# Two of four weight sums of a seven-product block scheme: from VectorE additions to accumulating transfers

## The chip, the cores and the metric

The kernel runs on one core of a Trainium2 chip. The metric is the device time of one execution in microseconds (us). The kernel before was run three times: 1967.50, 1963.14 and 1965.54 us, median 1965.54 us. One more execution was recorded by the hardware profiler; all rows below come from it.

The engines are named as the profile names them: PE (TensorE, matrix products), PEld (its weight loads), DVE (VectorE), ACT (ScalarE), POOL (GpSimd) and SP (SyncE, which here only issues transfers). A small q behind a name means the engine's queue of instructions rather than its datapath.

## What is computed

A decoder trunk of two layers on one sequence of 512 tokens with 1024 channels, in float32. Each layer adds three terms to x:

```
x += 0.5 * swiglu(rmsnorm(x), ffn1_w_in, ffn1_w_out)
x += mixer(rmsnorm(x))
x += 0.5 * swiglu(rmsnorm(x), ffn2_w_in, ffn2_w_out)

def _swiglu(x, w_in, w_out):
    gate, up = jnp.split(x @ w_in, 2, axis=-1)
    return (jax.nn.silu(gate) * up) @ w_out
```

The inner width of the feed-forward part is 2816. The mixers (a convolution beside sparse attention in the first layer, a short convolution beside stick-breaking attention in the second) are not touched by the change. A last norm ends the trunk. So there are four feed-forward parts, and the change lies in their second product, with `w_out`.

## The kernel before, in words

**Products in two halves.** Every float32 operand of a product is split into a rounded part and a rest (`split`, L87 to L94): ACT writes the rounded part (L90, or L93 with a factor), DVE subtracts it from the source (L91 or L94). `mm3` (L119 to L122) then issues three matmuls for each pair of 128 by 128 weights and a slab of activations. So each weight block costs one ACT pass, one DVE pass and a run of matmuls.

**The feed-forward part** (`ffn`, L248). Its inner width is 22 tiles of 128, taken in 11 pairs. `up(s)` computes one pair: four weight tiles of 512 KB come in by `load_w` (L103, three raw buffers, three buffers for each split half), 96 matmuls of 512 columns fill the banks `gu`, and DVE and ACT make the activation from them. The product with `w_out` takes three pairs at a time (`CHUNKS`), each in two halves of the output channels (`down(c0, n, q)`, L274). That is six calls of `seven` in each feed-forward part, 24 in the program. Between two calls stands at least one `up`. The last two pairs go through a plain product (`down_tail`).

**`seven`** (L211) multiplies a two by two block matrix in seven products instead of eight, Strassen's scheme in Winograd's form. The four weight blocks 11, 12, 21 and 22 of 384 KB each are loaded by SP into buffers `rb` (six of them, L220). DVE forms four weight sums in buffers `ws` (two of them) and in place:

```
s[1] = raw["21"] + raw["22"]         # L237, product 5
s[2] = s[1] + raw["11"]              # L238, product 6 (with the sign turned)
raw["21"] = raw["11"] + raw["21"]    # L240, product 7
s[2] = s[2] + raw["12"]              # L244, product 3
```

The products are written in the order 1, 2, 6, 7, 5, 4, 3; each splits its weights and issues 18 matmuls of 256 columns into the banks `px`, `py` and `pw`, and after each DVE adds the bank to the residual x (`taps`, L285).

**What sets the order of the work.** The program is written in the order above, but each engine's instructions are put in order at build time by a scheduler that simulates the engines: an instruction of lower rank (later in the program) goes ahead where a simulated engine has nothing earlier that is ready. Each engine then runs its list strictly in order. A buffer of a group (`rb`, `ws`, `raw`, `whi`, `wlo`) is handed out again when its last reader is done, and the loads of a later set are placed as soon as buffers are free. So SP, DVE and ACT work on the next call of `seven` while PE still works on the present one. POOL has little to do: in the feed-forward parts it adds squares for the next norm (`Norm.square`, L170), at the very start and beside the last plain products.

Of the kernel before, what the change touches and what calls it, by code (L numbers as in the profile page):

```python
# [11 lines left out]
ALU = mybir.AluOpType  # L12
# [22 lines left out]
S_11, S_21, S_22, S_T1, S_T3, S_T2, S_T4 = 1, 2, 3, 4, 5, 6, 7  # L35
# [17 lines left out]
def trunk(ctx: ExitStack, tc: tile.TileContext, a: dict, out: bass.AP):  # L53
    nc = tc.nc
    V, S, G, PE = nc.vector, nc.scalar, nc.gpsimd, nc.tensor
# [11 lines left out]
    def nm(s):  # L67
        n_name[0] += 1
        return f"{s}_{n_name[0]}"
# [17 lines left out]
    def split(hi, lo, src, scale=None):  # L87

        if scale is None:
            S.activation(hi, src, AF.Copy)  # L90
            V.tensor_tensor(lo, src, hi, ALU.subtract)  # L91
        else:
            S.activation(hi, src, AF.Copy, scale=scale)  # L93
            V.scalar_tensor_tensor(lo, src, scale, hi, op0=ALU.mult, op1=ALU.subtract)  # L94
# [24 lines left out]
    def mm3(o, wh, wl, xh, xl, start, stop, **kw):  # L119
        PE.matmul(o, wh, xh, start=start, stop=False, **kw)  # L120
        PE.matmul(o, wh, xl, start=False, stop=False, **kw)  # L121
        PE.matmul(o, wl, xh, start=False, stop=stop, **kw)  # L122
# [89 lines left out]
    def seven(ph, blocks, n, ops, taps):  # L212

        w = 2 * n * P
        raw = {}
        for b in ("11", "12", "22", "21"):
            raw[b] = ph.tile("rb", "rb", 768)[:, :w]
            nc.sync.dma_start(raw[b], blocks[b])  # L220
        s = {i: ph.tile("ws", "ws", 768)[:, :w] for i in (1, 2)}
        X, Y, W = (ph.bank(t, t) for t in ("px", "py", "pw"))

        def product(name, o, src, op, first, sign=None):
            hi = wsp.tile([P, 1024], F32R, tag="whi", name=nm("whi"))[:, :w]
            lo = wsp.tile([P, 1024], F32R, tag="wlo", name=nm("wlo"))[:, :w]
            split(hi, lo, src, sign)
            for k in range(n):
                for j in range(2):
                    sl = slice((j * n + k) * P, (j * n + k + 1) * P)  # L230
                    mm3(o[:, j * TH:(j + 1) * TH], hi[:, sl], lo[:, sl], *ops[k][op],
                        first and k == 0 and j == 0, k == n - 1, skip_group_check=True)
            taps(name, o)

        product("1", X, raw["11"], S_11, True)
        product("2", Y, raw["12"], S_21, True)
        V.tensor_tensor(s[1], raw["21"], raw["22"], ALU.add)  # L237
        V.tensor_tensor(s[2], s[1], raw["11"], ALU.add)  # L238
        product("6", X, s[2], S_T2, False, -1.0)
        V.tensor_tensor(raw["21"], raw["11"], raw["21"], ALU.add)  # L240
        product("7", W, raw["21"], S_T3, True)
        product("5", X, s[1], S_T1, False)
        product("4", W, raw["22"], S_T4, False)
        V.tensor_tensor(s[2], s[2], raw["12"], ALU.add)  # L244
        product("3", X, s[2], S_22, False)

    def ffn(norm, w_in, w_out, w_tail, nxt, ph, last=None):
# [30 lines left out]
        def down(c0, n, q):  # L278

            m0 = 4 * q  # L280

            def taps(m, o):
                r, c = {"1": (0, 0), "2": (0, 0), "6": (1, 0), "7": (1, 1), "5": (1, 1), "4": (1, 0), "3": (0, 1)}[m]
                x = xT[:, m0 + 2 * r:m0 + 2 * r + 2, c * TH:(c + 1) * TH]
                V.scalar_tensor_tensor(x, halves(o), -0.5 if r else 0.5, x, op0=ALU.mult, op1=ALU.add)  # L285

            w = 2 * n * P
            blocks = {b: w_out[q, i, :, 2 * c0 * P:2 * c0 * P + w] for i, b in enumerate(("11", "21", "12", "22"))}
            seven(ph, blocks, n, [act[c0 + k] for k in range(n)], taps)
# [569 lines left out]
    def early_w(n, c):  # L859
        sl = slice(c * T, (c + 1) * T)  # L860
        nc.sync.dma_start(first[n][:, sl], a["w1_in"][0][0, :, n, sl])
        return sp[n][0][:, sl], sp[n][1][:, sl], first[n][:, sl]

    order = {0: [(0, 0), (1, 0)], 2: [(0, 1)], 3: [(1, 1)]}
    for k in range(KD):
        nc.sync.dma_start(xT[:, k, :], a["x"][k])
        ws = [early_w(*nc_) for nc_ in order.get(k, ())]
# [175 lines left out]
```

## Time and profile before

| what | value |
|---|---|
| three runs | 1963.14 to 1967.50 us, median 1965.54 |
| profiled execution | 1965.56 us |
| its span, first to last instruction | 1963.8 us |
| PE busy | 1930.6 us (98%) |
| DVE busy | 1322.0 us (67%), 1973 instructions |
| ACT busy | 790.1 us (40%) |
| POOL busy | 104.1 us (5%), 112 instructions |
| moved by transfers | 178.02 MB, mean 91 GB/s |

How to read it: a busy share tells which engine has work all the time, not which one ends last at a given place. Matmuls are pipelined, so two neighbours overlap in the rows and the time of one is longer than the distance between two starts. The profiled execution lasted 1.76 us longer than its span.

### The profile page before, as it was taken

How to read it: one execution, taken by the hardware profiler on the slowest of the kernel's cores; microseconds unless marked ns; L12 is line 12 of the kernel's file. 1: busy time of each engine (PE TensorE's matmuls, PEld its weight loads, DVE VectorE, ACT ScalarE, POOL GpSimd, SP SyncE). 2: the span in 40 equal slices, each digit the busy share in tenths (PEclk: the TensorE clock that was granted, in tenths of full speed). 3: DMA queues.
4: the chain of work that ended last, by engine and by line, in shares of the span. 5: the costliest groups of instructions: out<-in, count | busy, mean ns of one | idle time of the engine just before them, and what ended most of it. 6: DMA issues, size and time to landing. Idle time of an engine off the chain costs nothing.

```text
span 1963.8 us, 25263 instructions
## 1 busy us (share of the span) xinstructions
PE 1930.6 (98%) x10128; PEld 1632.0 (83%) x10128; DVE 1322.0 (67%) x1973; ACT 790.1 (40%) x1129; POOL 104.1 (5%) x112
## 2 busy tenths in 40 slices
PE   8999999989999999999999999999999999999997
PEld 6888989878667888888988888888877888888896
DVE  6566757699986656666675666656578655666664
ACT  5333323436685433333343333334545433333333
POOL 2000000100232100000010000001000110000001
PEclk9999999999999999999999999999999999999999
DMA  6233331332100432323233333322321243232311
GB/s 220 94 91 102 92 102 52 100 103 82 43 1 28 150 97 84 113 82 117 86 111 96 97 97 98 98 80 75 94 67 55 77 143 97 84 114 81 117 52 54
DMA packets 53972, 178.02 MB, mean 91 GB/s; under 512 B 5984, under 2 KB 6368, under 8 KB 53856
## 3 DMA queue, kind: packets, MB, share of 16 engines
q1 hardware_dynamic: 53712, 176.29, 28.7%
q8 instruction: 79, 1.29, 0.3%
q14 instruction: 37, 0.30, 0.0%
q10 hardware_dynamic: 144, 0.14, 0.0%
HBM read 174.30 MB, written 2.10 MB: 90 GB/s over the span
## 4 chain that ended last, share of the span: by engine, by line
PE 97%; DVE 1%; ACT 1%; issue 0%; DMA 0%; DVEq 0%; SPq 0%; ACTq 0%
PE gu L120 16%; PE gu L121 16%; PE gu L122 16%; PE px L120 4%; PE px L122 4%; PE px L121 4%; PE ac L120 3%; PE ac L122 3%; PE ac L121 3%; PE pw L122 2%; PE pw L121 2%; PE pw L120 2%; PE fo L120 2%; PE fo L121 2%; PE fo L122 2%; PE mo L121 1%
## 5 line engine op out<-in xcount | busy, mean ns | idle before, releaser
L120 PE MATMUL gu<-xh,whi 128*128 128x512 f32 x1408 | 549.7, 391 | 8.3 <-ACT whi L90 6.1
L121 PE MATMUL gu<-xl,whi 128*128 128x512 f32 x1408 | 549.9, 391 | 0.0
L122 PE MATMUL gu<-xh,wlo 128*128 128x512 f32 x1408 | 546.4, 390 | 0.0
L90 ACT ACTIVATE whi<-raw 128x1024 fp32r<-128x1024 f32 (+2 forms) x256 | 268.9, 1051 | 565.3 <-PE gu L121 188.7
L91 DVE TENSOR_TENSOR wlo<-raw,whi 128x1024 fp32r<-128x1024 f32 (+2 forms) x256 | 312.8, 1222 | 55.0 <-ACT whi L90 51.0
L120 PEld LDWEIGHTS gu<-xh,whi 128*128 128x128 f32 x1408 | 265.5, 189 | 62.6 <-ACT whi L90 6.3
L122 PEld LDWEIGHTS gu<-xh,wlo 128*128 128x128 f32 x1408 | 265.2, 188 | 55.4
L121 PEld LDWEIGHTS gu<-xl,whi 128*128 128x128 f32 x1408 | 265.4, 189 | 53.8
L266 DVE TENSOR_TENSOR u<-gu,rstd 128x512 f32<-128x512 f32 x88 | 60.8, 691 | 264.6 <-PE gu L122 264.6
L90 ACT ACTIVATE whi<-rb 128x768 fp32r<-128x768 f32 x96 | 81.4, 848 | 266.5 <-PE gu L121 166.3
L263 DVE TENSOR_TENSOR g<-gu,rstd 128x512 f32<-128x512 f32 x88 | 60.8, 691 | 162.3 <-PE gu L122 155.8
L120 PE MATMUL px<-ah,whi 128*128 128x256 f32 x576 | 165.4, 287 | 1.6
L122 PE MATMUL px<-ah,wlo 128*128 128x256 f32 x576 | 163.4, 284 | 0.0
L121 PE MATMUL px<-al,whi 128*128 128x256 f32 x576 | 162.7, 282 | 0.0
L120 PEld LDWEIGHTS px<-ah,whi 128*128 128x128 f32 x576 | 108.8, 189 | 10.4 <-DVE xT L285 4.7
L120 PE MATMUL ac<-xh,whi 128*128 128x512 f32 x288 | 113.6, 395 | 1.5 <-ACT whi L90 1.5
L122 PE MATMUL ac<-xh,wlo 128*128 128x512 f32 x288 | 113.0, 393 | 0.0
L121 PE MATMUL ac<-xl,whi 128*128 128x512 f32 x288 | 112.8, 392 | 0.0
L121 PEld LDWEIGHTS px<-al,whi 128*128 128x128 f32 x576 | 108.7, 189 | 1.2
L122 PEld LDWEIGHTS px<-ah,wlo 128*128 128x128 f32 x576 | 108.6, 188 | 0.0
L170 POOL TENSOR_TENSOR ss<-sq,sq 128x512 f32<-128x512 f32 x7 | 12.5, 1787 | 1580.7 <-ACT sq L164 1580.7
L91 DVE TENSOR_TENSOR wlo<-rb,whi 128x768 fp32r<-128x768 f32 x96 | 91.7, 955 | 0.8
(316 smaller groups left out, 3245.8 us busy)
## 6 DMA issues: line engine op xcount, KB each, us to landing
raw<-in_w_in SPq DMA_DIRECT2D x174, 512.0 KB, 3.8
rb<-in_w_out SPq DMA_DIRECT2D x96, 384.0 KB, 3.1
raw<-in_cd_a SPq DMA_DIRECT2D x20, 512.0 KB, 3.6
raw<-in_w_tail SPq DMA_DIRECT2D x16, 512.0 KB, 4.0
raw<-in_ab_a SPq DMA_DIRECT2D x16, 512.0 KB, 3.5
raw<-in_ab_w_out SPq DMA_DIRECT2D x8, 512.0 KB, 3.7
raw<-in_cd_w_out SPq DMA_DIRECT2D x8, 512.0 KB, 3.6
xT<-in_x SPq DMA_DIRECT2D x8, 256.0 KB, 5.5
```

Source lines behind the costliest of these rows:

```text
L90: S.activation(hi, src, AF.Copy)
L91: V.tensor_tensor(lo, src, hi, ALU.subtract)
L120: PE.matmul(o, wh, xh, start=start, stop=False, **kw)
L121: PE.matmul(o, wh, xl, start=False, stop=False, **kw)
L122: PE.matmul(o, wl, xh, start=False, stop=stop, **kw)
L170: (V if self.n == KD - 1 else G).tensor_tensor(s2, self.ss[0], sq, ALU.add)
L263: V.tensor_tensor(g, ps[0], rstd, ALU.mult)
L266: V.tensor_tensor(u, ps[1], rstd, ALU.mult)
```

## The change

Sums 1 and 3 (the old L237 and L240) are no longer made by DVE. SP loads block 21 into a `ws` buffer and GpSimd issues a transfer that reads block 22 from memory and adds it to what lies in the buffer; for the other sum the same is done with 11 and 21. Block 21 itself is no longer kept in an `rb` buffer; the sum s[2] takes that place, and the two `ws` buffers hold the two transferred sums. The sums at the old L238 and L244 stay with DVE. The numbers of buffers stay as they are.

```diff
         raw = {}
-        for b in ("11", "12", "22", "21"):
+        for b in ("11", "12", "22"):
             raw[b] = ph.tile("rb", "rb", 768)[:, :w]
             nc.sync.dma_start(raw[b], blocks[b])
-        s = {i: ph.tile("ws", "ws", 768)[:, :w] for i in (1, 2)}
+        s = {}
+        for i, (b, b2) in {1: ("21", "22"), 3: ("11", "21")}.items():
+            s[i] = ph.tile("ws", "ws", 768)[:, :w]
+            nc.sync.dma_start(s[i], blocks[b])
+            G.dma_start(s[i], blocks[b2], accum_op=ALU.add)
+        s[2] = ph.tile("rb", "rb", 768)[:, :w]
         X, Y, W = (ph.bank(t, t) for t in ("px", "py", "pw"))
...
         product("1", X, raw["11"], S_11, True)
         product("2", Y, raw["12"], S_21, True)
-        V.tensor_tensor(s[1], raw["21"], raw["22"], ALU.add)
         V.tensor_tensor(s[2], s[1], raw["11"], ALU.add)
         product("6", X, s[2], S_T2, False, -1.0)
-        V.tensor_tensor(raw["21"], raw["11"], raw["21"], ALU.add)
-        product("7", W, raw["21"], S_T3, True)
+        product("7", W, s[3], S_T3, True)
         product("5", X, s[1], S_T1, False)
```

## Rows read from the trace of the kernel before

**Rows 1.** The page: span, busy time of the engines, and the chain that ended last

```profile
span 1963.8 us, 25263 instructions
...
PE 1930.6 (98%) x10128; PEld 1632.0 (83%) x10128; DVE 1322.0 (67%) x1973; ACT 790.1 (40%) x1129; POOL 104.1 (5%) x112
...
PE 97%; DVE 1%; ACT 1%; issue 0%; DMA 0%; DVEq 0%; SPq 0%; ACTq 0%
```

**Rows 2.** Windows: length, busy PE, PEld, DVE, ACT, POOL, clock, DMA share, GB/s

```profile
388.00:663.00 275.00, 264.42 (x1321) 204.43 (x1320) 230.61 (x483) 159.66 (x367) 47.69 (x72) 0.98 0.20 64
...
674.00:994.00 320.00, 319.61 (x1760) 278.58 (x1759) 209.87 (x272) 111.55 (x128) 0.00 (x0) 1.00 0.32 96
```

**Rows 3.** Groups by form: the four sums, count, busy us, mean ns, idle before

```profile
L238 DVE TENSOR_TENSOR ws<-ws,rb 128x768 f32<-128x768 f32 x24 | 23.0, 956 | 0.1
L240 DVE TENSOR_TENSOR rb<-rb,rb 128x768 f32<-128x768 f32 x24 | 22.9, 955 | 0.0
L237 DVE TENSOR_TENSOR ws<-rb,rb 128x768 f32<-128x768 f32 x24 | 22.9, 954 | 2.8 <-DMA rb<-in_w_out 2.8
L244 DVE TENSOR_TENSOR ws<-ws,rb 128x768 f32<-128x768 f32 x24 | 22.8, 952 | 0.0
```

**Rows 4.** The page, transfers issued: count, KB each, median us to landing

```profile
rb<-in_w_out SPq DMA_DIRECT2D x96, 384.0 KB, 3.1
```

**Rows 5.** The tile rb: all of its transfers, from issue to landing

```profile
DMA to landing us min/median/max: 3.0/3.1/8.1
```

**Rows 6.** Timeline of DVE in one set: start us, length us

```profile
106.32 0.95 DVE L91 TENSOR_TENSOR wlo<-rb,whi 128x768 fp32r<-128x768 f32 x1
...
108.99 0.95 DVE L91 TENSOR_TENSOR wlo<-ws,whi 128x768 fp32r<-128x768 f32 x1
109.86 0.68 DVE L285 SCALAR_TENSOR_TENSOR xT<-px,xT 128x512 f32<-128x512 f32 x1
...
111.92 0.95 DVE L237 TENSOR_TENSOR ws<-rb,rb 128x768 f32<-128x768 f32 x1
...
115.39 0.95 DVE L240 TENSOR_TENSOR rb<-rb,rb 128x768 f32<-128x768 f32 x1
116.26 1.22 DVE L91 TENSOR_TENSOR wlo<-raw,whi 128x1024 fp32r<-128x1024 f32 x1
...
117.99 0.95 DVE L238 TENSOR_TENSOR ws<-ws,rb 128x768 f32<-128x768 f32 x1
118.86 1.22 DVE L91 TENSOR_TENSOR wlo<-raw,whi 128x1024 fp32r<-128x1024 f32 x1
```

**Rows 7.** Timeline of the SP queue in the same set

```profile
107.29 0.33 SPq L220 DMA_DIRECT2D rb<-in_w_out  x1
```

**Rows 8.** Timeline of PE: first matmuls that read the rests of Rows 6

```profile
118.26 0.40 PE L122 MATMUL gu<-xh,wlo 128*128 128x512 f32 x1
...
123.73 0.39 PE L122 MATMUL gu<-xh,wlo 128*128 128x512 f32 x1
```

**Rows 9.** Timeline of ACT: product 6 of the next set splits its weights

```profile
139.18 0.85 ACT L93 ACTIVATE whi<-ws 128x768 fp32r<-128x768 f32 x1 [3.91 <-PE gu L121]
```

**Rows 10.** Waits: who for whom, us in total, times, longest

```profile
PEld px L120 <- DVE xT L285: 4.7, 16, 0.3
...
PE gu L120 <- DVE g L263: 2.2, 1, 2.2
```

**Rows 11.** Windows at the start (columns as in Rows 2)

```profile
15.00:20.00 5.00, 5.00 (x24) 4.14 (x23) 3.15 (x6) 3.26 (x5) 3.67 (x2) 1.00 1.03 415
...
35.00:40.00 5.00, 5.00 (x16) 3.91 (x16) 4.88 (x10) 1.90 (x4) 0.00 (x0) 0.66 0.31 105
```

**Rows 12.** Tile ss, POOL's additions: ns min/median/max, first and last start

```profile
L170 POOL TENSOR_TENSOR ss<-ss,sq x35: 1277/1393/2157, 13.2 to 1944.1; 128x512 f32<-128x512 f32 x35
```

**Rows 13.** Window over one set (columns as in Rows 2)

```profile
101.90:122.00 20.10, 20.00 (x148) 18.77 (x147) 19.80 (x26) 9.03 (x10) 0.00 (x0) 1.00 0.31 93
```

## The prediction

> **What bounds the kernel now.** I read the page first, for the chain that ended last: PE makes 97% of it and is busy for 1930.6 of 1963.8 us, while DVE, which the change relieves, makes 1% of the chain although it is busy for two thirds of the time [rows 1]. Then I cut the span into stages by windows. The change lies in the four feed-forward stages, and in the one shown PE is busy for 319.61 of 320 us at full clock; the other two undisturbed ones look the same, and the first has 2 us idle near its start. The first mixer, which the change does not touch, holds the largest idle stretch, 275 minus 264.42 = 10.6 us [rows 2]. So in the stages of the change nothing but matmuls sets the end, and their number does not change. Last I read the groups for the sums, and one set's timeline on DVE, SP, PE and ACT for who waits for whom.
>
> **What the change removes.** L237 and L240 go, 24 instructions each: 22.9 + 22.9 = 45.8 us of DVE time [rows 3]. In a set DVE has a dense stretch, 19.80 busy of 20.10 us [rows 13], and there the next set's sums stand at 111.92, 115.39 and 117.99 [rows 6], some 21 us ahead of product 6 of that set, whose split starts at 139.18 [rows 9]. They are done early, between other work, and PE does not wait for them. Value on the path: 0. It could be a little more. PE waits 16 times, 4.7 us in all, for an eviction of px by DVE, and once 2.2 us at the start [rows 10]. The eviction in question, at 109.86, stands ahead of both removed sums in DVE's queue [rows 6], so I take 0 and keep 4.7 + 2.2 = 6.9 us as the end of the range.
>
> **What it adds, SP.** A set has five plain loads instead of four: 24 more issues of 0.33 us on SP [rows 7]. The two `ws` loads now wait for the two `ws` buffers. In the set shown the buffer that takes the place of product 7's source is read last at 106.32 + 0.95 = 107.27, and that of product 5 at 108.99 + 0.95 = 109.94 [rows 6]. SP today also waits there: it issues an `rb` load at 107.29 [rows 7] and then waits for raw buffers. So the new waits fall into a stretch in which SP waits anyway; behind them stand loads for `up` that need a raw buffer released by the DVE instruction at 116.26 or later. Cost 0.
>
> **The transfers.** With 384 KB = 393,216 bytes each [rows 4], a set adds one plain load and two accumulating ones, 24 x 3 x 0.393 = 28.3 MB. The engines that move data are busy for 0.31 to 0.32 of the time there [rows 2, 13]; three more beside four `rb` loads and the weights of `up` leave that below a half even if an accumulation counts twice. Cost 0 in the steady sets.
>
> **An accumulating transfer's own latency** is in no row. Below, it cannot beat the plain load of the same bytes, 3.1 us [rows 5]. Above, I let it read source and destination one after the other, 2 x 3.1, and add the longest of POOL's additions, 2.2 us [rows 12], for the time that POOL needs to write it out: 8.4 us. I take 5.5 us, near the middle, as both ends rest on the same row. The Trainium skill, "DMA: Bandwidth & Descriptors", section "Anatomy of one DMA", gives 2.0 us plus bytes over 436 GB/s for a transfer issued by GpSimd, an estimate of 2.9 us here, by which the sum would be the same.
>
> **The chain that replaces the two sums.** A buffer is free at 107.3, the plain load lands 3.1 us later at 110.4, the accumulation at 110.4 + 5.5 = 115.9. Product 6 needs s[2] at 139.18. For data alone there are 28 us to spare, less one addition. The s[3] chain starts 2.7 us later, and only splits read it. The new wait that matters is L238: it waits for the transfer inside DVE's strict queue, and everything behind it waits too. At its present place, 117.99, a transfer of up to 117.99 - 110.4 = 7.6 us is free. Behind it stands the rest of a raw tile (118.86 + 1.22 = 120.08) that PE first reads at 123.73 [rows 8]; that adds 3.6 us. So free to 11.2 us, and I cost the wait at 0. If the scheduler puts L238 where L240 stood, 115.39, only 5.0 us are free ahead of it, and behind it stands the rest ready at 116.26 + 1.22 = 117.48 that PE reads at 118.26 [rows 8], 0.8 us more, plus the 0.95 us of the removed L237: free to 6.7 us.
>
> **POOL.** 48 issues. In the steady sets it has nothing else (0.00 busy) [rows 2]. An addition of squares queued behind an accumulation waits for that load to land; they meet at the start only, and perhaps at a stage's end.
>
> **The start** is the one place where transfers are scarce: 1.03 share, 415 GB/s in 15 to 20 us [rows 11]. The first set asks for three more transfers there, 1.18 MB / 415 GB/s = 2.8 us, ahead of weights for `up`. Between 0 and 2.8 us; I take 1 us, since PE is busy for all of that window and works on tiles already loaded.
>
> **Sum.** 1965.56 (the profiled execution: span 1963.8 plus 1.76 outside it; the median of the runs is 1965.54) + 0 + 1 = 1966.5 us. About 0.2%, 3.9 us, is what a measurement of this kernel can tell from no change.
>
> **Rivals.**
>
> Slower, L238 in the wrong place: the order is fixed by a simulated timeline, which has to guess the accumulation's landing. If it guesses low, L238 moves up to 115.39 and DVE stands still there, with evictions and rests behind it. It decides from 6.7 us of latency upward; at 8.4 us it costs 1.7 us a set, 24 x 1.7 = 41 us, 2007 us, and half of that, some 1986, for a latency between. For it: DVE has 0.3 us of air in 20 us [rows 13]. Against: L237 met the landing of a plain load late only for 2.8 us in all [rows 3], so the simulated landings are about right. Chance 0.23.
>
> Slower, the start: the full 2.8 us come late and PE's clock falls again, as it did to 0.66 in 35 to 40 us after the 2.2 us wait [rows 10, 11]; a window of 5 us at 0.66 loses at most 1.7 us. 1965.6 + 2.8 + 1.7 = 1970.1, a band of 1969.5 to 1972. Chance 0.10.
>
> Slower, DVE holds up POOL: POOL's additions take 1.28 to 2.16 us for one size [rows 12], so something beside them slows them. If writing out the accumulation had to wait for a pause of DVE, it would begin only when DVE stops at L238. DVE would then stand for 3.1 to 6.2 us at 117.99, less the 3.6 us of slack: up to 2.6 x 24 = 62 us, 2028 us. The Trainium skill, "GPSIMD Engine Reference", section "Specifications", says that GpSimd's memory interfaces contend with DVE instructions of two inputs, which nearly all of DVE's here are; "SBUF — State Buffer", section "Who interferes with whom", limits that to GpSimd instructions that read the memory, and infers that writing descriptors is not among them. By the first the sum would be this rival's, by the second the forecast's; POOL's additions do read, so the row agrees with both. Chance 0.04.
>
> Faster: DVE's lighter load moves its list up and PE's 6.9 us of waits go, wholly or mostly: 1965.6 - 6.9 = 1958.7, a band of 1958.7 to 1961.5. For it: all of them wait on DVE [rows 10]. Against: the evictions stand ahead of the removed sums. Chance 0.13.
>
> **How the numbers follow.** No change has 0.50, faster 0.13, slower 0.23 + 0.10 + 0.04 = 0.37. The range reaches from 1960, inside the faster band, to 1990, past the middle of the first rival; what lies outside is some 0.05 below, 0.08 of the first rival and 0.03 of the third.
>
> **What would show it.** DVE at 1925 instructions and about 1276 us busy, PE's busy time unchanged; POOL with 48 more instructions; 206 MB moved. L238 without idle time before it, or with less than its slack, and feed-forward windows with PE still over 99% busy. A row "DVE ws L238 waits for a transfer" of tens of us, with PE idle after it, would prove the forecast wrong; so would a first `gu` tile that waits for `raw` in the first 40 us.

## The result and the profile after

The changed kernel takes 2038.12 us (median of 4 runs, 2024.40 to 2041.69) against 1965.56 us for the kernel before (4 runs, 1963.14 to 1967.50): a ratio of 1.0357, 95% interval 1.0308 to 1.0406. It is slower by some 72 us, outside the range that was given. A ratio, here and below, takes in all runs and is not the quotient of the medians beside it, as runs of one kernel can differ by 10 to 21 us with their mean granted clock (experiment 8: 1963.3 to 1964.8 us at 0.992, 1985.3 to 1985.8 at 0.980). The profiled execution took 2036.96 us, its span is 71.4 us longer than the one before (2035.2 against 1963.8), and the rows below are read against that.

The page of the changed kernel: span, busy time of the engines, the chain that ended last, and at the end three rows of the transfers (queue, count, KB each, median us from issue to landing).

```profile
span 2035.2 us, 25368 instructions
...
PE 1958.8 (96%) x10128; PEld 1649.5 (81%) x10128; DVE 1279.2 (63%) x1925; ACT 790.2 (39%) x1129; POOL 149.6 (7%) x160
...
PE 79%; DVE 9%; DMA 8%; issue 3%; ACT 0%; DVEq 0%; SPq 0%; POOLq 0%; ACTq 0%
...
rb<-in_w_out SPq DMA_DIRECT2D x72, 384.0 KB, 6.3
ws<-in_w_out SPq DMA_DIRECT2D x48, 384.0 KB, 3.0
ws<-in_w_out POOLq DMA_DIRECT2D x48, 384.0 KB, 7.5
```

Against [rows 1], DVE has lost its 48 instructions and 43 us of work, as the diff says, yet it went from 1% of the chain to 9%, and the transfers from 0% to 8%. The chain is the place to look first: an engine can do less and hold up more. The plain `rb` loads take 6.3 us where they took 3.1 [rows 4], beside accumulations of 7.5 us.

The waits of the changed kernel name the place (who waits at which line, for whom: us in total, times, longest). Line numbers have moved by a few: L242 is the sum for s[2], which was L238, and L288 is the eviction, which was L285.

```profile
DVE rb L242 <- DMA ws<-in_w_out: 82.7, 24, 6.5
...
PE gu L122 <- DVE wlo L91: 37.7, 18, 3.3
...
PE fo L122 <- DVE wlo L91: 4.2, 1, 4.2
```

DVE waits at the s[2] sum in each of the 24 sets, 82.7 / 24 = 3.45 us a time, until s[1] has been accumulated. TensorE then waits for the rest (`wlo`) of a weight tile that DVE hadn't split: 37.7 + 4.2 = 41.9 us. Neither of the `wlo` rows was there before.

One set of the changed kernel, from its timeline (start us, length us; in brackets the idle time ahead of the instruction and what ended it):

```profile
109.64 3.00 SPq L224 DMA_DIRECT2D ws<-in_w_out  x2
...
112.20 0.68 DVE L288 SCALAR_TENSOR_TENSOR xT<-px,xT 128x512 f32<-128x512 f32 x1
...
113.12 0.86 POOL L225 DMA_DIRECT2D ws<-in_w_out  x1 [87.31 <-DVE xT L288]
...
116.27 0.68 DVE L288 SCALAR_TENSOR_TENSOR xT<-px,xT 128x512 f32<-128x512 f32 x1
...
119.63 0.96 DVE L242 TENSOR_TENSOR rb<-ws,rb 128x768 f32<-128x768 f32 x1 [2.68 <-DMA ws<-in_w_out]
...
120.51 1.22 DVE L91 TENSOR_TENSOR wlo<-raw,whi 128x1024 fp32r<-128x1024 f32 x1
...
121.78 0.50 PE L122 MATMUL gu<-xh,wlo 128*128 128x512 f32 x1 [1.18 <-DVE wlo L91]
```

DVE is done with the eviction of product 5 at 116.95 and comes to the s[2] sum 3.8 us after POOL began to issue the accumulation, which lands 6.5 us after that. The sum therefore stands for 2.68 us, the split that TensorE needs next stands behind it, and TensorE waits for 1.18 us. So of this wait 2.68 - 1.18 = 1.50 us were free. In the kernel before, this place in DVE's queue, behind the same eviction and ahead of the same split, was L240's (115.39 and 116.26 in [rows 6]); the row ahead of those two was

```profile
114.79 0.69 DVE L285 SCALAR_TENSOR_TENSOR xT<-px,xT 128x512 f32<-128x512 f32 x1
```

The 41.9 us are not all of it. The windows of two feed-forward stretches of the changed kernel (columns as in [rows 2]):

```profile
35.00:365.00 330.00, 321.06 (x1737) 278.47 (x1738) 198.04 (x258) 110.60 (x128) 8.73 (x10) 0.98 0.37 106
...
686.00:1025.00 339.00, 326.51 (x1750) 282.34 (x1749) 198.39 (x266) 110.72 (x127) 10.15 (x12) 0.98 0.39 110
```

They now have 9 and 12.5 us in which PE does nothing, where [rows 2] has 0.4, and the granted clock is 0.98 where it was 1.00. Pieces of 5 us show where the clock goes:

```profile
220.00:225.00 5.00, 3.06 (x8) 2.44 (x9) 5.00 (x6) 0.21 (x1) 0.00 (x0) 0.74 0.67 178
225.00:230.00 5.00, 5.00 (x21) 4.08 (x21) 1.31 (x3) 1.36 (x2) 0.00 (x0) 0.92 0.63 212
...
260.00:265.00 5.00, 2.46 (x11) 1.73 (x10) 3.60 (x4) 1.06 (x1) 0.00 (x0) 0.84 0.72 174
265.00:270.00 5.00, 5.00 (x20) 4.02 (x19) 1.96 (x3) 0.00 (x0) 0.00 (x0) 0.82 0.80 245
...
780.00:785.00 5.00, 2.12 (x10) 1.45 (x9) 3.62 (x4) 1.06 (x1) 0.00 (x0) 1.00 0.62 154
```

The first two pairs are the sets in which TensorE had waited 2.2 us (to 221.94) and 2.5 us (to 263.55): part of these pieces ran at 1.2 instead of 2.4 GHz. In the sets where it waited 1.2 us (to 121.78 and 160.47) the rows stay at 1.00. The length of the wait alone doesn't decide it: after 2.9 us (to 783.53, the last row) the clock stayed at 1.00, in the next 5 us too, and after 1.8 us (to 990.07) it was 0.66 in the next 5 us. Over the span the mean granted clock is 0.980 against 0.994, which is 2035.2 x 0.020 - 1963.8 x 0.006 = 28.9 us. Waits and clock make 41.9 + 28.9 = 70.8 of the 71.4 us.

Not all of the clock's part stands behind those waits. Counted in pieces of 5 us over the whole span, the clock falls behind 11 of the 19 waits for `wlo`, which is 22 us together. Most of the rest, some 7 us, lies in the first mixer, where the change has no sums; one stretch of it, in the kernel before and then in the changed one:

```profile
550.00:600.00 50.00, 47.65 (x234) 31.57 (x233) 39.55 (x127) 41.99 (x111) 15.26 (x30) 0.97 0.00 1
...
550.00:600.00 50.00, 46.22 (x210) 31.54 (x209) 36.80 (x118) 36.26 (x92) 16.64 (x31) 0.86 0.00 1
```

So about 41.9 + 22 = 64 of the 71 us are tied to the waits for `wlo`; why the mixer's clock is lower too is not shown.

### The profile page after: what moved, and what is told of

It reads as the page before. It is cut to its first block, busy times and chain, and to the rows that moved or that the text cites. A ratio compares the mean times of both kernels' runs of the same rounds, so it can differ in the third digit from the quotient of the medians.

```text
span 2035.2 us, 25368 instructions
## 1 busy us (share of the span) xinstructions
PE 1958.8 (96%) x10128; PEld 1649.5 (81%) x10128; DVE 1279.2 (63%) x1925; ACT 790.2 (39%) x1129; POOL 149.6 (7%) x160
## 4 chain that ended last, share of the span: by engine, by line
PE 79%; DVE 9%; DMA 8%; issue 3%; ACT 0%; DVEq 0%; SPq 0%; POOLq 0%; ACTq 0%
PE gu L122 16%; PE gu L120 16%; PE gu L121 16%; DMA ws<-in_w_out 8%; PE ac L122 3%; PE ac L120 3%; PE ac L121 3%; DVE wlo L91 3%; DVE xT L288 2%; PE fo L122 2%; PE fo L120 2%; PE fo L121 1%; PE mo L121 1%; PE mo L120 1%; PE pt L397 1%
## 5 line engine op out<-in xcount | busy, mean ns | idle before, releaser
L122 PE MATMUL gu<-xh,wlo 128*128 128x512 f32 x1408 | 559.2, 397 | 37.8 <-DVE wlo L91 37.7
L120 PE MATMUL gu<-xh,whi 128*128 128x512 f32 x1408 | 556.3, 396 | 7.7 <-ACT whi L90 6.3
L121 PE MATMUL gu<-xl,whi 128*128 128x512 f32 x1408 | 556.2, 395 | 0.0
L120 PEld LDWEIGHTS gu<-xh,whi 128*128 128x128 f32 x1408 | 270.1, 192 | 63.1 <-ACT whi L90 6.8
L225 POOL DMA_DIRECT2D ws<-in_w_out x48 | 42.1, 883 | 1218.7 <-DVE xT L288 1039.0
```

Of the source, the lines that this page charges most:

```text
L225: G.dma_start(s[i], blocks[b2], accum_op=ALU.add)
```

## The experiments

Theory A says that DVE, standing at the s[2] sum, makes the loss; theory B, that the accumulating transfers themselves do. The kernel before took 1964.8 us (23 runs) beside the first four, 1965.99 (22) beside the next four and 1965.42 (13) beside the last two.

**1. The sum in place.** Only the tile that s[2] is written to differs, so all transfers stay:

```
-        s[2] = ph.tile("rb", "rb", 768)[:, :w]
+        s[2] = raw["11"]
```

> Edit: the changed kernel, but the sum s[2] is written in place over block 11, so it can only run after product 1 has split block 11, some 10 us later in DVE's list; both accumulating transfers stay. Theory A (the loss is DVE standing still at this sum until the accumulation of s[1] lands, with PE's weight rests behind it): DVE no longer waits for a ws transfer (under 5 us in all instead of 82.7), PE's wait for wlo in gu goes from 37.7 us to under 3, and the time is 1960 to 1970 us. Theory B (the loss is the transfers themselves: 28 MB more, and plain loads that land in 6.3 instead of 3.1 us beside the accumulations): the same bytes move, so the time stays at 2025 to 2042 us.

Measured: 1968.75 us, ratio 1.0030 (1.0006 to 1.0053); the profiled execution took 1963.72. The sum can now start only behind product 1's split of block 11, late in DVE's queue, and no row of DVE waiting for `ws` is left. The page still says, of this kernel's transfers:

```profile
rb<-in_w_out SPq DMA_DIRECT2D x72, 384.0 KB, 6.4
...
ws<-in_w_out POOLq DMA_DIRECT2D x48, 384.0 KB, 7.5
```

The slow transfers are all there, and the time is 1 to 10 us above the kernel before, not 72. That is theory A, and theory B falls.

**2. The sum on POOL.**

```
-        V.tensor_tensor(s[2], s[1], raw["11"], ALU.add)
+        G.tensor_tensor(s[2], s[1], raw["11"], ALU.add)
```

> Edit: the changed kernel, but the sum s[2] = s[1] + block 11 is made by POOL; its place in the program stays. POOL then stands and waits for the accumulation, and DVE has one instruction less. Theory A: 1960 to 1972 us, and no DVE wait for a ws transfer. Theory B: 2025 to 2042 us as in the changed kernel.

Measured: 1972.43 us, ratio 1.0028 (1.0011 to 1.0044), profiled execution 1964.37. Among its waits:

```profile
POOL rb L242 <- DMA ws<-in_w_out: 91.8, 24, 5.6
```

The same wait, even longer, on an engine that has only its issues for the next set behind it here: TensorE's waits on `wlo` are gone. The median lies 0.4 us above what theory A had said, far from theory B.

**3 and 4. One accumulation alone.** Both edits are shown against the kernel before. First only product 7's sum by accumulation; s[1] is written over block 21:

```
-        s = {i: ph.tile("ws", "ws", 768)[:, :w] for i in (1, 2)}
+        s = {3: ph.tile("ws", "ws", 768)[:, :w]}
+        nc.sync.dma_start(s[3], blocks["11"])
+        G.dma_start(s[3], blocks["21"], accum_op=ALU.add)
+        s[1], s[2] = raw["21"], ph.tile("ws", "ws", 768)[:, :w]
...
-        V.tensor_tensor(raw["21"], raw["11"], raw["21"], ALU.add)
-        product("7", W, raw["21"], S_T3, True)
+        product("7", W, s[3], S_T3, True)
```

> Edit: only the sum for product 7 is made by an accumulating transfer; s[1] and s[2] are made by DVE from plain loads as before. No DVE sum reads an accumulated buffer. Theory A: no loss, 1960 to 1972 us. Theory B: the bytes beyond the kernel before are 18.9 MB instead of 28.3, and half of the accumulations stay, so some 45 to 65% of the 72 us, 1998 to 2012 us.

Measured: 1978.67 us, ratio 1.0091 (1.0066 to 1.0116). Then only s[1] by accumulation, product 7's sum on DVE again:

```
-        s = {i: ph.tile("ws", "ws", 768)[:, :w] for i in (1, 2)}
+        s = {1: ph.tile("ws", "ws", 768)[:, :w]}
+        nc.sync.dma_start(s[1], blocks["21"])
+        G.dma_start(s[1], blocks["22"], accum_op=ALU.add)
+        s[2] = ph.tile("ws", "ws", 768)[:, :w]
...
-        V.tensor_tensor(s[1], raw["21"], raw["22"], ALU.add)
```

> Edit: only s[1] is made by an accumulating transfer; the sum for product 7 is made by DVE as before, s[2] by DVE from the accumulated s[1]. Theory A: DVE waits at s[2] in all 24 sets as in the changed kernel, and the loss stays for the most part: 2005 to 2040 us. Theory B: the same bytes as with the sum for product 7 alone, 1998 to 2012 us; the two kernels with one accumulation each would be equal.

Measured: 1977.45 us, ratio 1.0067 (1.0052 to 1.0081). Both missed what theory A had said, in opposite directions, and both lie below what theory B had said. The waits of the kernel with s[1] alone:

```profile
DVE ws L240 <- DMA ws<-in_w_out: 46.7, 23, 2.7
...
PE px L120 <- DVE xT L287: 14.6, 19, 1.0
```

DVE waits 2.0 us a set here and TensorE doesn't wait for a `wlo` at all. The s[2] sum (L240 here) stands two places later than in the changed kernel, behind the split that TensorE needs next; experiments 7, 9 and 10 come back to that:

```profile
114.67 1.21 DVE L91 TENSOR_TENSOR wlo<-raw,whi 128x1024 fp32r<-128x1024 f32 x1
...
118.45 0.96 DVE L240 TENSOR_TENSOR ws<-ws,rb 128x768 f32<-128x768 f32 x1 [1.97 <-DMA ws<-in_w_out]
```

What TensorE waits for is an eviction of px, here and with s[3] alone (16.5 us, 21 times). The timeline of the kernel with s[3] alone shows why (the sum L240 there is s[1]'s):

```profile
109.06 0.95 DVE L240 TENSOR_TENSOR rb<-rb,rb 128x768 f32<-128x768 f32 x1
109.92 0.68 DVE L287 SCALAR_TENSOR_TENSOR xT<-px,xT 128x512 f32<-128x512 f32 x1
```

The planner has put a sum of the next set directly ahead of the eviction that product 5 waits for; in [rows 6] the sum came behind it. So these 12 to 14 us seem to have another cause than the 71, and experiment 8 tests that for the kernel with s[1] alone.

**5. Transfer without the addition.** It leaves out the addition of block 22 to s[1] and of 21 to s[3]; the order of the instructions is the same on every engine.

```
-            G.dma_start(s[i], blocks[b2], accum_op=ALU.add)
+            G.dma_start(s[i], blocks[b2])
```

> The two POOL transfers of a set stay, at the same places in every queue and with the same bytes, but write plainly instead of adding: the additions of block 22 to s[1] and of 21 to s[3] are left out. Theory A (DVE stands at the head of its queue until s[1] has landed, and what that wait has beyond some 2 us reaches TensorE) makes the time follow the landing. If it is the adding that makes 7.5 us of a transfer, the plain one lands in 3 to 5 us as SP's do, the DVE wait falls from 82.7 us to under 30 and the time to 1962-1980 us. If it is the route over POOL or the transfers beside it, it lands in 7 to 8 us as before and the time stays at 2020-2045 us. Theory B (the bytes moved cost, whatever waits) gives 2020-2045 us in either case.

Measured: 1981.16 us, ratio 1.0081 (1.0068 to 1.0094). From its waits, and from its page:

```profile
DVE rb L242 <- DMA ws<-in_w_out: 37.0, 23, 3.2
...
PE gu L122 <- DVE wlo L91: 5.4, 8, 1.1
```

```profile
ws<-in_w_out POOLq DMA_DIRECT2D x48, 384.0 KB, 5.0
```

Without the adding a transfer that POOL issues, two a set, takes 5.0 instead of 7.5 us. With 37.0 / 23 = 1.6 us a set, DVE's wait is about the 1.5 us that were free in the set above, and TensorE's waits on `wlo` fall from 41.9 us to 5.4 and 0.8 (`fo`). Theory A had said a wait of DVE under 30 us and 1962 to 1980 us; both are missed by a little, and theory B by some 40 us.

**6. The same transfers, s[1] earlier.** s[1] goes into one of the six `rb` buffers, where SP loads ahead, and s[2] takes its `ws` buffer:

```
-            s[i] = ph.tile("ws", "ws", 768)[:, :w]
+            t = "rb" if i == 1 else "ws"
+            s[i] = ph.tile(t, t, 768)[:, :w]
...
-        s[2] = ph.tile("rb", "rb", 768)[:, :w]
+        s[2] = ph.tile("ws", "ws", 768)[:, :w]
```

> s[1] is accumulated in one of the six rb buffers and s[2] takes the ws buffer that s[1] had; both accumulating transfers stay. SP can then load s[1] a set ahead, as it does the plain blocks, so POOL's accumulation should land before DVE reaches the s[2] sum. Theory A: the DVE wait of 82.7 us falls under 20 us, the TensorE waits of 37.7 us on wlo go, granted clock back at 0.99, time 1962-1976 us. Theory B (transfers): 2015-2045 us, since the same transfers run.

Measured: 1975.31 us, ratio 1.0038 (1.0014 to 1.0061), 1963.24 at the lowest. Among its waits:

```profile
DVE ws L243 <- DMA rb<-in_w_out: 8.2, 6, 2.8
```

POOL issues s[1]'s accumulation 0.86 us ahead of px's eviction in that set (at 109.75, the eviction at 110.61), where the changed kernel did so 0.92 us behind it. The wait of 82.7 us is down to 8.2, and of TensorE's waits on `wlo` 0.4 us are left. The clock is not back at 0.99, as had been expected: it is 0.986 in the profiled execution of 1976.41 us. What that has beyond 1963 doesn't lie in the sets but in the first mixer, where there are no sums:

```profile
550.00:570.00 20.00, 19.39 (x72) 12.92 (x71) 13.86 (x41) 12.86 (x29) 4.11 (x8) 0.69 0.00 0
```

**7. A longer wait.** The two accumulations change places, so that s[1] lands where s[3] did:

```
-        for i, (b, b2) in {1: ("21", "22"), 3: ("11", "21")}.items():
+        for i, (b, b2) in {3: ("11", "21"), 1: ("21", "22")}.items():
```

> The two accumulations change places: s[3] first, s[1] second, everything else as in the changed kernel. s[1] then lands where s[3] did, some 3.8 us later (119.61 and 123.46 us in one set). Theory A: the DVE wait of a set grows from 3.45 to 6.5-7.3 us, each set costs TensorE 3 to 3.9 us more, 24 sets 72 to 94 us: 2095-2140 us. Theory B (same transfers, same bytes): 2024-2042 us.

Measured: 1994.24 us (2 runs), ratio 1.0145 (1.0127 to 1.0162). Faster than the changed kernel, with a longer wait, so both theories missed. Its waits, and DVE in the same set:

```profile
DVE rb L242 <- DMA ws<-in_w_out: 111.3, 23, 5.9
...
PE gu L122 <- DVE wlo L91: 5.3, 12, 0.9
```

```profile
119.26 1.21 DVE L91 TENSOR_TENSOR wlo<-raw,whi 128x1024 fp32r<-128x1024 f32 x1
120.39 0.68 DVE L288 SCALAR_TENSOR_TENSOR xT<-pw,xT 128x512 f32<-128x512 f32 x1
126.24 0.96 DVE L242 TENSOR_TENSOR rb<-ws,rb 128x768 f32<-128x768 f32 x1 [5.17 <-DMA ws<-in_w_out]
```

With s[1] later, the planner has moved the sum two places down, behind the split that TensorE needs next. DVE then stands for 111.3 / 23 = 4.8 us, but the next split behind it is needed only one gu pass later (24 matmuls that start 0.23 us apart, 5.5 us). So theory A needs the place as well as the length: A'. The 28 us that are left lie mostly outside the sets: the mean clock is 0.983, some 22 us more lost than before, and 17 of them in the first mixer:

```profile
550.00:600.00 50.00, 48.06 (x162) 31.48 (x162) 29.11 (x96) 29.11 (x73) 10.62 (x22) 0.62 0.00 1
```

**8. The eviction.** The kernel of experiment 4, with product 7's sum written over block 11, so that it can't start ahead of the eviction:

```
-        V.tensor_tensor(raw["21"], raw["11"], raw["21"], ALU.add)
-        product("7", W, raw["21"], S_T3, True)
+        V.tensor_tensor(raw["11"], raw["11"], raw["21"], ALU.add)
+        product("7", W, raw["11"], S_T3, True)
```

> As the kernel in which only s[1] is accumulated (1977.5 us), but product 7's sum on DVE is written over block 11 instead of block 21, so that it can't start before product 1's split and can't stand ahead of the eviction of the set before. Theory (that kernel's 12 us come from the sum that stands ahead of px's eviction, so that product 5 waits about 0.7 us longer in some 20 sets): the TensorE waits at px fall from 14.6 us to 4-7 us and the time to 1962-1969 us, with DVE's wait of about 2 us a set on s[1] still there. Rival (that wait of 2 us, or the transfer, is what costs the 12 us): 1974-1981 us.

Measured: 1964.75 us, ratio 1.0034 (1.0005 to 1.0064), profiled execution 1963.34. No row of TensorE waiting for px's eviction is left, and DVE still waits for s[1] (the second row is the part that shows no releaser; together 2.3 us a set):

```profile
DVE ws L240 <- DMA ws<-in_w_out: 35.2, 15, 3.5
...
DVE ws L240 <- issue: 19.3, 8, 2.6
```

So the 12 us of experiment 4 came from the sum ahead of the eviction, and the lone accumulation, with the s[2] sum behind the split, shows no cost in its profile. For experiment 3 the same cause is likely from its rows, but was not tested.

**9 and 10. A delay, one place apart.** POOL copies n columns of s[1]'s plain load into a spare tile before it issues the accumulation, with n = 320 in one kernel and 384 in the other. Nothing else in the two texts differs:

```
+    spare = const.tile([P, 384], F32, name="spare")
...
-            G.dma_start(s[i], blocks[b2], accum_op=ALU.add)
+            m = min(w, n)
+            G.tensor_copy(spare[:, :m], s[i][:, :m]) if i == 1 else None
+            G.dma_start(s[i], blocks[b2], accum_op=ALU.add)
```

With 320 columns the sum keeps its place. With 384 the planner puts it one place later, behind the split.

> As the changed kernel, with one more instruction a set: POOL copies 320 columns of s[1]'s plain load into a spare tile that nothing reads, before it issues the accumulation of s[1], so that s[1] lands some 0.5 to 1 us later. The s[2] sum keeps its place in DVE's queue, directly ahead of the split of the weights that TensorE reads next. Theory A' (wait times place: of a wait ahead of that split about 2.68 - 1.18 = 1.5 us are free, the rest goes to TensorE): 0.5 to 1 us more in each of 21 sets, TensorE's waits on wlo at 50-65 us instead of 42, time 2045-2075 us. Rival (only the mean wait counts, wherever it stands): 2045-2075 us as well.

> The same with a copy of 384 columns instead of 320. s[1] lands no earlier than in the kernel with 320, but the s[2] sum now stands one place later in DVE's queue, behind the split that TensorE reads next and ahead of pw's eviction. Theory A': the DVE wait is still 2.5 to 3.5 us a set (60 to 85 us in all), the next split behind it is needed only a gu pass later (24 matmuls of 0.227 us, 5.4 us), so TensorE's waits on wlo fall under 8 us and the time to 1962-1988 us. Rival (the length of the wait counts, wherever it stands): 2030-2075 us.

Measured: 2047.15 us with 320 columns, ratio 1.0404 (1.0378 to 1.0431), and 1974.70 us with 384, ratio 1.0038 (1.0025 to 1.0051). Waits, then DVE in one set, with 320 columns:

```profile
DVE rb L242 <- DMA ws<-in_w_out: 100.2, 23, 6.9
...
PE gu L122 <- DVE wlo L91: 47.6, 20, 3.6
```

```profile
115.88 0.68 DVE L288 SCALAR_TENSOR_TENSOR xT<-px,xT 128x512 f32<-128x512 f32 x1
120.60 0.96 DVE L242 TENSOR_TENSOR rb<-ws,rb 128x768 f32<-128x768 f32 x1 [4.04 <-DMA ws<-in_w_out]
121.48 1.22 DVE L91 TENSOR_TENSOR wlo<-raw,whi 128x1024 fp32r<-128x1024 f32 x1
```

And with 384 columns:

```profile
DVE rb L242 <- DMA ws<-in_w_out: 68.0, 24, 5.7
```

```profile
115.21 0.69 DVE L288 SCALAR_TENSOR_TENSOR xT<-px,xT 128x512 f32<-128x512 f32 x1
115.81 1.22 DVE L91 TENSOR_TENSOR wlo<-raw,whi 128x1024 fp32r<-128x1024 f32 x1
119.15 0.96 DVE L242 TENSOR_TENSOR rb<-ws,rb 128x768 f32<-128x768 f32 x1 [2.11 <-DMA ws<-in_w_out]
120.02 0.69 DVE L288 SCALAR_TENSOR_TENSOR xT<-pw,xT 128x512 f32<-128x512 f32 x1
```

A wait of 2.8 us a set behind the split costs TensorE nothing that its waits show, and the time is 72 us less; 4.4 us ahead of the split cost 47.6 us there. The time with 320 columns was forecast by A' and by the rival alike; that with 384 decides for A' (1962 to 1988 us) against the rival (2030 to 2075). The two delays are not quite equal, though "no earlier" had been expected: counted from the eviction of px, the sum starts after 3.94 us in the one set and after 4.72 in the other, so s[1] lands 0.8 us earlier there with 384 columns. That doesn't make the difference: counted from the place ahead of the split, which takes 1.1 us, s[1] is 2.8 + 1.1 = 3.9 us late with 384 columns, more than the 3.45 us of the changed kernel, where TensorE waited for 41.9 us. The size from A' was too high for the first: 4.4 - 1.5 = 2.9 us in 23 sets would be 66 us, and the rows have 47.6 and 3.3 more in another group, 50.9. The 1.5 us that are free in one set are not the same in every set.

No version was faster than the kernel before by more than the measurement can tell.

## Why the prediction was wrong

**The step that failed** is the s[2] sum's wait, taken at 0 on the ground that "At its present place, 117.99, a transfer of up to 117.99 - 110.4 = 7.6 us is free". The present place was not the place to cost. The set above runs 2.34 us later than the one in [rows 6] (its px eviction stands at 112.20 instead of 109.86). In the times of that set the sum came to the head of the queue at 116.95 - 2.34 = 114.61, which is 3.4 us ahead of 117.99: it stands where L240 stood, as the first rival had it, and earlier than 115.39 as L237 is gone. The plain load landed as assumed, at 109.64 + 2.9 - 2.34 = 110.2 (110.4 was assumed), the accumulation 1.4 us later than assumed, at 113.12 + 6.5 - 2.34 = 117.3 instead of 115.9. It took both: at 117.99 data of 117.3 would have been in time, and in this set data of 115.9 would have held up DVE but not TensorE, which loses from 116.1 on (the 1.50 us that were free). Experiments 7 and 10 move the place, experiment 5 shortens the transfer, and each takes most of TensorE's waits away.

**The latency** was taken as 5.5 us, between 3.1 and 8.4. It is 5.0 to 5.2 us where one accumulation a set runs (experiments 3, 4, 8) and 7.5 where two run side by side, 8.8 at most; in experiment 6, where s[1]'s starts 2.1 us ahead of the other, 5.2 and 7.9. Inside the bounds, but the value came from a middle; that two of them and two `rb` loads are under way at once was in no term.

**The first rival** had the mechanism and the very place: the sum where L240 stood, DVE standing with a rest behind it. Its threshold of 6.7 us was too high: the 0.95 us of the removed L237 bring DVE to the sum earlier, but not TensorE to the rest later. For the rest to be there at 118.26 the sum has to start by 115.39 + 0.8 = 116.2, so it decides from 116.2 - 110.4 = 5.8 us, just above the 5.5 us of the forecast. Then 8.4 us would have cost 2.6 us a set, 62 us, 2028 us. So it is luck that its end, 41 us, is what TensorE's new waits come to, 41.9. What it lacked is TensorE's clock after such waits, 22 us here: the clock was priced in the second rival only, at the start, though [rows 11] had shown it fall after one wait of 2.2 us. At the 1.7 us that were lost there, 24 sets would have added 41 us to the rival's 2007, an estimate of 2048 us, above what was measured. Its chance, 0.23, rested on the sentence that a plain `rb` load was met late for 2.8 us in all [rows 3]; how well the planner knows SP's plain loads says nothing of how well it knows POOL's accumulations.

**Removed sums, 0:** right. Experiments 1 and 6 have them removed as well, without the wait, and run at 1962.6 and 1963.2 us at the lowest, against 1962.5 to 1962.9 of the kernel before. **Transfers, 0:** right for the sum, as the same bytes in experiment 1 cost nothing on the path that its waits show, though the `rb` loads beside them became slower. **SP, 0:** nothing speaks against it. **The start, 1 us:** about right in size by luck; the first `g` came at 35.55 instead of 33.99 us, but through the s[2] sum, which stood for 1.98 us inside the chain that makes `rstd`, and not through bandwidth.

**DVE holds up POOL:** refuted. POOL issued the accumulation at 113.12 in 0.86 us, in the midst of DVE's dense stretch, and before DVE stopped at 116.95 part of its data had moved. Between 113.9 and 116.9 us the queue of POOL's transfers has these packets, MB and share of the 16 engines:

```profile
q0 software_dynamic: 49, 0.15, 43.7%
```

In experiment 1 DVE doesn't stop at the sum, and the accumulations land in 7.5 us all the same. That agrees with the Trainium skill, "SBUF — State Buffer", section "Who interferes with whom", which infers that writing descriptors is not held up by such instructions. **Faster:** didn't come, though its condition did: the row of px waiting for DVE's eviction [rows 10] is gone. But that row is PEld's, not PE's: PE itself stood for 1.6 us in all ahead of these px matmuls before the change and for 1.6 us after it, so of the 4.7 us there was next to nothing to gain.

## What to carry to other kernels

A wait in an in-order queue is costed by two numbers: how late the data come at the place where the wait *will* stand, and when the instruction behind it is needed. Where a planner sets the order, the places of the instructions that stay move when others go, so price the new wait at the earliest place it can take, and then at each place up to the present one. And where TensorE is the bound, add to its repeated waits what the clock can lose after them, from a row of the same trace; here it lost some 1.7 us or more after 11 of 19 waits and nothing after the others.

## What was not expected

- Accumulating transfers of 384 KB took 5.0 to 5.2 us alone and 7.5 us in pairs; plain ones that POOL issued in pairs took 5.0 us and SP's 3.0 to 3.1. Beside the pairs, SP's `rb` loads went from 3.1 to 6.3 us, beside the plain pairs of experiment 5 to 5.2; beside a lone one they stayed at 3.2.
- POOL's own time for an issue was 0.88 us with the addition (42.1 us for 48) and 0.54 us without.
- The first mixer, which no version touches, ran at different clocks: in 550 to 600 us 0.97 before the change, 0.86 after it, 0.62 in experiment 7; experiment 6 has 0.69 in 550 to 570, experiment 8 has 0.83 there and 1.00 in the next 20 us. Why stays open. In the profiles of experiments 6 and 7 it is most of what they have beyond the kernel before, and it may be what lifts other ratios above to 1.003 and 1.004.
